# Low halves of every second weight chunk built by an accumulating transfer instead of a VectorE subtract

## The chip, the cores and the metric

One core of a Trainium2 chip runs the kernel. The metric is the device time of one execution in microseconds (us). The engines have short names in the rows: PE is TensorE (matmul), PEld its weight load, DVE is VectorE, ACT is ScalarE, POOL is GpSimd, SP is SyncE. A transfer is issued by an engine's queue (SPq, ACTq, POOLq) and carried out by the 16 DMA engines that all queues share.

## The reference

One decoder block on 256 tokens (16 meta tokens ahead of them), width 2048, in float32, with one output per token. Cut to what matters:

```
hn = rms_norm(h, norm_mix_g)
u, gb, gc, v, ga, gbr = split(hn @ w_in)
y_a = (multi_scale_pool(u) @ pool_w) * pool_scale        # 4 groups of 512 channels
y_b = (gb * causal_conv(gc * v, conv_w)) @ conv_out_w
h   = h + (sigmoid(ga + b) * y_a + sigmoid(gbr + b) * y_b) @ w_o
gate, up = split(rms_norm(h, norm_ffn_g) @ w_gate_up)    # hidden width 5632
h   = h + (silu(gate) * up) @ w_down
out = rms_norm(h, norm_final_g)[16:]
```

## The kernel before

All weights stand in memory as one stream of 528 chunks, in the order of use. A chunk is 128 partitions by 1024 float32 (512 KB), or eight tiles of 128x128. Each chunk goes through three pools: `raw` as it was loaded, `hi`, the same values rounded to float32r, and `lo = raw - hi`, the rest, also float32r. A product in nearly full precision is then three matmuls: activation hi times weight hi, activation hi times weight lo, activation lo times weight hi. In `mm_rows` a chunk is two blocks of 128x512, each used for two halves of the tokens, so 12 matmuls, and the second matmul of a chunk is the first to read `lo`. In `mm_flat` (the first stages) it is the third of 24.

`next_block` and `next_tile` hand out the tiles. At the first tile of chunk c they call `advance(c)`, which issues the load of chunk c + 4 on SP's queue and the split of chunk c + 2: ScalarE casts raw to hi (line 115), VectorE subtracts hi from raw into lo (line 116). With three buffers in `whi` and `wlo`, the split of chunk c + 2 takes the buffers of chunk c - 1, so its cast waits until TensorE has done its last matmul on chunk c - 1. `wraw` has five buffers.

The stages, in chunks: w_in in columns (0 to 127; pool and convolution branches), then gates, pool_w and conv_out_w in blocks of rows, w_o, gate and up of the FFN up to chunk 439, and w_down in four groups of 22 chunks (440 to 527), whose first group is `first` in line 451. After each group the sums in PSUM are taken over by VectorE and ScalarE (sigmoid, square, transposes and casts), and in w_down GpSimd multiplies the sum `hn` by `gf` (line 469) after the first three of the four groups. GpSimd also issues five transfers in its queue: `hn`, four of `sp` (line 384), `gf` (line 455).

Every engine takes its instructions in order: what stands behind a waiting instruction on its queue waits too. The order on each queue is made when the kernel is built, from the order in which the code records instructions.

Of the kernel before, what the change touches and what calls it, by code (L numbers as in the profile page):

```python
# [8 lines left out]
F32 = mybir.dt.float32  # L9
F32R = mybir.dt.float32r  # L10
AF = mybir.ActivationFunctionType
ALU = mybir.AluOpType
PSUM = bass.MemoryType.PSUM

P = 128
# [14 lines left out]
CH = 8  # L30
HEAD = CH // 2
LOADS_AHEAD = 4
SPLITS_AHEAD = 2

# [1 line left out]
BC = BW * P  # L38
# [15 lines left out]
def block_kernel(ctx: ExitStack, tc: tile.TileContext, xT, xn, gfin, consts, spread, weights, out):  # L54
# [4 lines left out]
    nc = tc.nc  # L59

    one = ctx.enter_context(tc.tile_pool(name="one", bufs=1))
    apool = ctx.enter_context(tc.tile_pool(name="apool", bufs=1))
    wraw = ctx.enter_context(tc.tile_pool(name="wraw", bufs=5))
    whi = ctx.enter_context(tc.tile_pool(name="whi", bufs=3))
    wlo = ctx.enter_context(tc.tile_pool(name="wlo", bufs=3))
    ps = ctx.enter_context(tc.tile_pool(name="ps", bufs=8, space=PSUM))
    scope = ExitStack()
    spool = scope.enter_context(tc.tile_pool(name="spool", bufs=KT))
# [13 lines left out]
    def bank():  # L82
        return ps.tile([P, 512], F32, name="acc")
# [8 lines left out]
    dummy = bank()  # L92
    for _ in range(WARM):
        nc.tensor.matmul(out=dummy[:, :P], lhsT=ones, rhs=ones, start=True, stop=True)
# [3 lines left out]
    raws, splits = {}, {}  # L98
# [9 lines left out]
    def split_weights(c, parts=1):  # L108
        raw = raws.pop(c)
        hi = whi.tile([P, CH * P], F32R, name="hi")  # L110
        lo = wlo.tile([P, CH * P], F32R, name="lo")
        step = CH * P // parts
        for s in range(0, CH * P, step):
            q = slice(s, s + step)
            nc.scalar.copy(out=hi[:, q], in_=raw[:, q])  # L115
            nc.vector.tensor_tensor(out=lo[:, q], in0=raw[:, q], in1=hi[:, q], op=ALU.subtract)  # L116
        splits[c] = hi, lo
# [3 lines left out]
    def advance(c):  # L121
        while state["loaded"] < min(c + LOADS_AHEAD + 1, n_chunks):
            load(state["loaded"])
            state["loaded"] += 1
        while state["split"] < min(c + SPLITS_AHEAD + 1, n_chunks):
            split_weights(state["split"])
            state["split"] += 1
# [29 lines left out]
    def rows(acts, held=0, n=None, before=None):  # L157

        ps_ = [bank() for _ in range(NB)]
        n = n or len(acts)
        for k in range(n - held):
            if before and k == n - BW:
                before()
            blk = next_block()
            for b in range(NB):
                mm_rows(ps_[b], acts[k], b, blk, k == 0, k == n - 1)
        kept = []
        for k in range(n - held, n):  # L170
            kept.append(next_block())
            mm_rows(ps_[0], acts[k], 0, kept[-1], k == 0, k == n - 1)
        for k, blk in zip(range(n - held, n), kept):
            mm_rows(ps_[1], acts[k], 1, blk, k == 0, k == n - 1)
        return ps_
# [32 lines left out]
    def binary(o, a, b, op=ALU.mult):  # L208
        nc.vector.tensor_tensor(out=o, in0=a, in1=b, op=op)
        return o  # L210
# [81 lines left out]
    for c in range(KT * HEAD // CH):  # L292
        k0 = c * CH // HEAD
        k1 = k0 + CH // HEAD
        xsp += [wide(xall[:, k, :], col(C_GMIX, k)) for k in range(k0, k1)]
        split_weights(c, 2 if c == 0 else 1)
        state["split"] = c + 1
        for k in range(k0, k1):
            for m in range(HEAD):
                cc, i = divmod(state["tile"], CH)  # L300
                state["tile"] += 1
                hi, lo = splits[cc]
                hi, lo = hi[:, i * P : (i + 1) * P], lo[:, i * P : (i + 1) * P]
                p, a, f, last = heads[m][:, : SEQ + w0], xsp[k], NMETA - w0, k == KT - 1
                nc.tensor.matmul(out=p, lhsT=hi, rhs=a[:, 0, f:], start=k == 0, stop=False)  # L305
                nc.tensor.matmul(out=p, lhsT=hi, rhs=a[:, 1, f:], start=False, stop=False)  # L306
                nc.tensor.matmul(out=p, lhsT=lo, rhs=a[:, 0, f:], start=False, stop=last)  # L307
# [57 lines left out]
    tmr = scope.enter_context(tc.tile_pool(name="tmr", bufs=1))  # L365
# [4 lines left out]
    def turn_s(c):  # L370
        turn(s_rows.pop(c), c, lambda j, p: ss.append(narrow(p, "a")))

    def gates(bias):
        gs = []
        for b, p in enumerate(rows(xsp)):
            g = slot("x", [P, BC])
            nc.vector.scalar_tensor_tensor(out=g, in0=p, scalar=r1p[:, b : b + 1], in1=bias, op0=ALU.mult, op1=ALU.add)
            nc.scalar.activation(out=g, in_=g, func=AF.Sigmoid)
            gs.append(g)
        return gs  # L380

    for c in range(NC):
        sp = tmr.tile([P, 3, BC], F32, name="sp", tag="sp", bufs=2)
        nc.gpsimd.dma_start(out=sp, in_=spread[:, :, c * BC : (c + 1) * BC])
        ga = gates(sp[:, 0, :])
        for g in ga:
            binary(g, g, sp[:, 2, :])
        if c > 0:
            turn_s(c - 1)
        gb = gates(sp[:, 1, :])  # L390
        for b, p in enumerate(rows(pooled[c * GT : (c + 1) * GT])):
            binary(ga[b], p, ga[b])
        for b, p in enumerate(rows(zs)):
            binary(gb[b], p, gb[b])
            binary(gb[b], gb[b], ga[b], ALU.add)
        s_rows[c] = gb
# [4 lines left out]
    tmr = scope.enter_context(tc.tile_pool(name="tmr", bufs=1))  # L401
# [60 lines left out]
    for c in range(NC):  # L462
        q = slice(c * BC, (c + 1) * BC)
        last = c == NC - 1
        for b, p in enumerate(first if c == 0 else rows(acts, HELD if last else 0)):
            h = hn[:, b, q]
# [21 lines left out]


HELD = 6  # L490
WARM = 14


# [70 lines left out]
```

## Time and profile before

| | |
|---|---|
| median of 2 runs | 1497.62 us (1497.62 to 1497.63) |
| the profiled execution, its own time | 1497.58 us |
| its span, first to last instruction | 1495.8 us |
| TensorE busy, share of the span | 1484.4 us, 99% |
| VectorE, ScalarE, GpSimd busy | 861.2, 657.2, 16.2 us |

The profiled execution takes 1.8 us more than its span, for what lies ahead of the first and behind the last instruction. The busy share is not the limit by itself; which wait ends last is read from the chain of waits and from the order of time.

### The profile page before, as it was taken

What the parts mean: (1) busy time and instruction counts of PE and PEld (TensorE: products, weight loads), DVE (VectorE), ACT (ScalarE), POOL (GpSimd) and SP (SyncE); (2) the same over time, 40 slices, a digit from 0 to 9 for tenths busy, and PEclk for the clock granted to TensorE, in tenths of its full rate; (3) what the DMA queues carried; (4) which work ended last, traced back from release to release, by engine and by line L of the source; (5) the groups of instructions that cost most, each with busy time, mean ns of one, the idle gap of its engine ahead of it and who ended that gap; (6) DMA issues with size and microseconds to landing.
All of it is one profiled execution on the core that took longest, in us unless ns stands there. A gap on an engine that the chain in (4) does not pass through costs nothing.

```text
span 1495.8 us, 19632 instructions
## 1 busy us (share of the span) xinstructions
PE 1484.4 (99%) x7800; PEld 1278.0 (85%) x7800; DVE 861.2 (58%) x1020; ACT 657.2 (44%) x785; POOL 16.2 (1%) x19
## 2 busy tenths in 40 slices
PE   9999999999999999999999999999999999999997
PEld 9999999999888888888888888888888888888886
DVE  7986666666555555555564555555555554445454
ACT  6444444444444444444553444444444444344343
POOL 0000000000000000000000000000000000000000
PEclk9999999999999999999999999999999999999999
DMA  8555555555765655555556555565555556556653
GB/s 340 185 179 187 185 183 184 185 185 187 231 209 183 212 184 189 191 186 191 186 169 202 192 183 194 185 189 193 192 187 189 191 185 222 183 196 197 191 192 125
DMA packets 79291, 288.76 MB, mean 193 GB/s; under 512 B 8784, under 2 KB 9040, under 8 KB 78944
## 3 DMA queue, kind: packets, MB, share of 16 engines
q1 hardware_dynamic: 77472, 279.61, 56.9%
q0 software_dynamic: 1152, 6.33, 1.3%
q8 instruction: 61, 1.00, 0.3%
q10 hardware_dynamic: 576, 1.57, 0.3%
q14 instruction: 30, 0.25, 0.0%
HBM read 285.38 MB, written 2.10 MB: 192 GB/s over the span
## 4 chain that ended last, share of the span: by engine, by line
PE 99%; ACT 0%; DMA 0%; DVE 0%; issue 0%; POOLq 0%; ACTq 0%
PE acc L155 24%; PE acc L154 24%; PE acc L153 24%; PE acc L185 6%; PE acc L187 6%; PE acc L186 6%; PE acc L179 4%; PE acc L180 2%; PE acc L242 1%; PE acc L305 1%; PE acc L307 1%; PE acc L306 1%; DMA cst<-consts 0%; ACT hi L115 0%; ACT hg L486 0%
## 5 line engine op out<-in xcount | busy, mean ns | idle before, releaser
L116 DVE TENSOR_TENSOR lo<-raw,hi 128x1024 fp32r<-128x1024 f32 (+1 forms) x529 | 648.0, 1225 | 584.2 <-ACT hi L115 581.0
L115 ACT CAST hi<-raw 128x1024 fp32r<-128x1024 f32 (+1 forms) x529 | 555.8, 1051 | 800.2 <-PE acc L155 561.7
L153 PE MATMUL acc<-hi,hp 128*128 128x512 f32 x704 | 274.7, 391 | 0.3 <-ACT hi L115 0.3
L154 PE MATMUL acc<-lo,hp 128*128 128x512 f32 x704 | 273.7, 389 | 0.0
L155 PE MATMUL acc<-hi,hp 128*128 128x512 f32 x704 | 273.7, 389 | 0.0
L153 PE MATMUL acc<-hi,act 128*128 128x512 f32 x640 | 248.8, 390 | 0.5 <-ACT hi L115 0.5
L154 PE MATMUL acc<-lo,act 128*128 128x512 f32 x640 | 248.7, 389 | 0.0
L155 PE MATMUL acc<-hi,act 128*128 128x512 f32 x640 | 248.4, 389 | 0.0
L185 PE MATMUL acc<-xp,hi 128*128 128x258 f32 (+3 forms) x704 | 200.5, 285 | 0.0
L187 PE MATMUL acc<-xp,lo 128*128 128x258 f32 (+3 forms) x704 | 199.8, 284 | 0.0
L186 PE MATMUL acc<-xp,hi 128*128 128x258 f32 (+3 forms) x704 | 198.4, 282 | 0.0
L155 PEld LDWEIGHTS acc<-hi,hp 128*128 128x128 f32 x704 | 132.1, 188 | 27.7
L153 PEld LDWEIGHTS acc<-hi,hp 128*128 128x128 f32 x704 | 132.1, 188 | 27.4 <-ACT hi L115 0.5
L154 PEld LDWEIGHTS acc<-lo,hp 128*128 128x128 f32 x704 | 132.2, 188 | 27.1
L153 PEld LDWEIGHTS acc<-hi,act 128*128 128x128 f32 x640 | 120.0, 188 | 25.9 <-ACT hi L115 1.0
L154 PEld LDWEIGHTS acc<-lo,act 128*128 128x128 f32 x640 | 120.1, 188 | 25.1
L155 PEld LDWEIGHTS acc<-hi,act 128*128 128x128 f32 x640 | 120.1, 188 | 24.7
L186 PEld LDWEIGHTS acc<-xp,hi 128*128 128x128 f32 x704 | 132.9, 189 | 0.0
L185 PEld LDWEIGHTS acc<-xp,hi 128*128 128x128 f32 x704 | 132.2, 188 | 0.7
L187 PEld LDWEIGHTS acc<-xp,lo 128*128 128x128 f32 x704 | 132.4, 188 | 0.0
L155 PE MATMUL acc<-hi,xp 128*128 128x512 f32 x256 | 101.7, 397 | 0.0
L154 PE MATMUL acc<-lo,xp 128*128 128x512 f32 x256 | 101.1, 395 | 0.0
(107 smaller groups left out, 1005.9 us busy)
## 6 DMA issues: line engine op xcount, KB each, us to landing
raw<-weights SPq DMA_DIRECT2D x527, 512.0 KB, 3.4
sp<-spread POOLq DMA_DIRECT2D x4, 768.0 KB, 6.7
hn<-xn POOLq DMA_DIRECT2D x1, 2048.0 KB, 9.8
xall<-xT SPq DMA_DIRECT2D x7, 272.0 KB, 6.8
gf<-gfin POOLq DMA_DIRECT2D x1, 1024.0 KB, 7.9
out<-hg SPq DMA_DIRECT2D x2, 512.0 KB, 2.6
out<-hg ACTq DMA_DIRECT2D x2, 512.0 KB, 3.5
raw<-weights ACTq DMA_DIRECT2D x2, 256.0 KB, 4.1
```

The source lines that it names most:

```text
L115: nc.scalar.copy(out=hi[:, q], in_=raw[:, q])
L116: nc.vector.tensor_tensor(out=lo[:, q], in0=raw[:, q], in1=hi[:, q], op=ALU.subtract)
L153: nc.tensor.matmul(out=p, lhsT=a[:, 0, t], rhs=hi, start=first, stop=False)
L154: nc.tensor.matmul(out=p, lhsT=a[:, 0, t], rhs=lo, start=False, stop=False)
L155: nc.tensor.matmul(out=p, lhsT=a[:, 1, t], rhs=hi, start=False, stop=last)
L179: nc.tensor.matmul(out=p, lhsT=hi, rhs=a[:, :, off : off + SEQ], start=first, stop=False)
L180: nc.tensor.matmul(out=p[:, :SEQ], lhsT=lo, rhs=a[:, 0, off : off + SEQ], start=False, stop=last)
L185: nc.tensor.matmul(out=p, lhsT=hi, rhs=a[:, 0, off : off + n], start=first, stop=False)
L186: nc.tensor.matmul(out=p, lhsT=hi, rhs=a[:, 1, off : off + n], start=False, stop=False)
L187: nc.tensor.matmul(out=p, lhsT=lo, rhs=a[:, 0, off : off + n], start=False, stop=last)
L242: nc.tensor.transpose(out=p[:, q : q + P], in_=src[b][:, f], identity=ident)
L305: nc.tensor.matmul(out=p, lhsT=hi, rhs=a[:, 0, f:], start=k == 0, stop=False)
```

## The change

For odd chunks from chunk 16 on (`ADD_FROM`), the low part is made in another way. ScalarE casts raw to hi as before, then ScalarE writes lo = -hi, and GpSimd's queue issues a transfer that reads the same chunk from memory a second time and adds it onto lo. Even chunks, and the first 16, keep VectorE's subtract. The splits now run three chunks ahead, `whi` and `wlo` have four buffers, `wraw` four, and `sp` one buffer instead of two.

```
-SPLITS_AHEAD = 2
+SPLITS_AHEAD = 3
...
-    wraw = ctx.enter_context(tc.tile_pool(name="wraw", bufs=5))
-    whi = ctx.enter_context(tc.tile_pool(name="whi", bufs=3))
-    wlo = ctx.enter_context(tc.tile_pool(name="wlo", bufs=3))
+    wraw = ctx.enter_context(tc.tile_pool(name="wraw", bufs=4))
+    whi = ctx.enter_context(tc.tile_pool(name="whi", bufs=4))
+    wlo = ctx.enter_context(tc.tile_pool(name="wlo", bufs=4))
...
         hi = whi.tile([P, CH * P], F32R, name="hi")
         lo = wlo.tile([P, CH * P], F32R, name="lo")
+        if c >= ADD_FROM and c % 2:
+
+            nc.scalar.copy(out=hi, in_=raw)
+            nc.scalar.activation(out=lo, in_=hi, func=AF.Copy, scale=-1.0)
+            nc.gpsimd.dma_start(out=lo, in_=weights[c], accum_op=ALU.add)
+            splits[c] = hi, lo
+            return
         step = CH * P // parts
...
-        sp = tmr.tile([P, 3, BC], F32, name="sp", tag="sp", bufs=2)
+        sp = tmr.tile([P, 3, BC], F32, name="sp", tag="sp", bufs=1)
...
+ADD_FROM = 16
```

GpSimd's queue before, from the load of `hn` to the end (L384 and L455 are the loads of `sp` and `gf`, L469 the multiplications in w_down; a row with x6 is six such instructions):

```order
L403 DMA hn<-xn 128x4096
L384 DMA sp<-spread 128x3x512 x4
L455 DMA gf<-gfin 128x2048
L469 TENSOR_TENSOR hg<-hn,gf 128x512 x6
```

The same queue after, from the last load of `sp` (now L391) to the end (L116 is the accumulating transfer, L462 the load of `gf`, L476 the multiplications):

```order
L391 DMA sp<-spread 128x3x512
L116 DMA lo<-weights 128x1024 x122
L462 DMA gf<-gfin 128x2048
L116 DMA lo<-weights 128x1024 x11
L476 TENSOR_TENSOR hg<-hn,gf 128x512 x2
L116 DMA lo<-weights 128x1024 x11
L476 TENSOR_TENSOR hg<-hn,gf 128x512 x2
L116 DMA lo<-weights 128x1024 x11
L476 TENSOR_TENSOR hg<-hn,gf 128x512 x2
L116 DMA lo<-weights 128x1024 x10
```

256 accumulating transfers now stand in a queue that had five other transfers and six multiplications. Counted from the front, those of chunks up to 439 stand ahead of the load of `gf`, and that of chunk 441 right behind it. Those of chunks 463, 485 and 507 stand right behind a pair of multiplications.

ScalarE's queue after, at the end of the first group of w_down (L122 casts an even chunk, L114 casts an odd one, L115 writes its negative into lo, L475 squares a finished sum):

```order
L122 CAST hi<-raw 128x1024
L114 CAST hi<-raw 128x1024
L475 ACTIVATE junk,part<-hn 128x512
L115 ACTIVATE lo<-hi 128x1024
L475 ACTIVATE junk,part<-hn 128x512
L122 CAST hi<-raw 128x1024
L114 CAST hi<-raw 128x1024
L115 ACTIVATE lo<-hi 128x1024
```

Per pair of chunks ScalarE has three instructions on weights instead of two. At the end of a group, work on the finished sums can stand between an odd chunk's cast and its negative; that is so in 16 places for sigmoids and squares.

## Rows read from the trace of the kernel before

**Rows 1.** The page: span, busy time, TensorE's clock, queues, the chain that ended last.
```profile
span 1495.8 us, 19632 instructions
...
PE 1484.4 (99%) x7800; PEld 1278.0 (85%) x7800; DVE 861.2 (58%) x1020; ACT 657.2 (44%) x785; POOL 16.2 (1%) x19
...
q1 hardware_dynamic: 77472, 279.61, 56.9%
...
PE 99%; ACT 0%; DMA 0%; DVE 0%; issue 0%; POOLq 0%; ACTq 0%
```

**Rows 2.** The page's costliest groups: the subtract and the cast of a chunk.
```profile
L116 DVE TENSOR_TENSOR lo<-raw,hi 128x1024 fp32r<-128x1024 f32 (+1 forms) x529 | 648.0, 1225 | 584.2 <-ACT hi L115 581.0
L115 ACT CAST hi<-raw 128x1024 fp32r<-128x1024 f32 (+1 forms) x529 | 555.8, 1051 | 800.2 <-PE acc L155 561.7
```

**Rows 3.** Windows, instructions of line 115 alone: start:end, length, ScalarE busy (casts), clock, DMA.
```profile
115.00:375.00 260.00, 95.58 (x91) 1.00 0.56 185
...
785.00:1240.00 455.00, 173.06 (x164) 1.00 0.58 190
```

**Rows 4.** Order of time, TensorE in the FFN: start, length (us), line, operands.
```profile
1015.83 0.39 PE L155 MATMUL acc<-hi,hp 128*128 128x512 f32 x1
1016.05 0.39 PE L153 MATMUL acc<-hi,hp 128*128 128x512 f32 x1
1016.28 0.39 PE L154 MATMUL acc<-lo,hp 128*128 128x512 f32 x1
```

**Rows 5.** Order of time, ScalarE in the same stretch.
```profile
1016.25 1.05 ACT L115 CAST hi<-raw 128x1024 fp32r<-128x1024 f32 x1 [1.67 <-PE acc L155]
1018.97 1.05 ACT L115 CAST hi<-raw 128x1024 fp32r<-128x1024 f32 x1 [1.67 <-PE acc L155]
```

**Rows 6.** Order of time, VectorE in the same stretch.
```profile
1017.34 1.22 DVE L116 TENSOR_TENSOR lo<-raw,hi 128x1024 fp32r<-128x1024 f32 x1 [1.49 <-ACT hi L115]
```

**Rows 7.** The page's transfers: size each, median us from issue to landing.
```profile
raw<-weights SPq DMA_DIRECT2D x527, 512.0 KB, 3.4
sp<-spread POOLq DMA_DIRECT2D x4, 768.0 KB, 6.7
hn<-xn POOLq DMA_DIRECT2D x1, 2048.0 KB, 9.8
...
gf<-gfin POOLq DMA_DIRECT2D x1, 1024.0 KB, 7.9
```

**Rows 8.** The tile sp alone: landing, shortest, median, longest.
```profile
DMA to landing us min/median/max: 5.7/6.7/11.2
```

**Rows 9.** Windows, all engines; the last three columns are clock, DMA share, GB/s.
```profile
10.00:20.00 10.00, 10.00 (x85) 10.00 (x85) 10.00 (x17) 10.00 (x20) 0.00 (x0) 1.00 1.03 416
...
1450.00:1496.00 46.00, 37.33 (x165) 30.59 (x163) 20.58 (x28) 16.11 (x20) 0.00 (x0) 0.93 0.39 137
```

**Rows 10.** Order of time, GpSimd in the FFN's end and w_down.
```profile
1246.85 0.55 POOL L455 DMA_DIRECT2D gf<-gfin  x1 [751.86 <-DVE gs L447]
1309.08 3.54 POOL L469 TENSOR_TENSOR hg<-hn,gf 128x512 f32<-128x512 f32 x2 [61.68 <-DVE hn L209]
1367.96 3.53 POOL L469 TENSOR_TENSOR hg<-hn,gf 128x512 f32<-128x512 f32 x2 [55.35 <-DVE hn L209]
1427.81 3.54 POOL L469 TENSOR_TENSOR hg<-hn,gf 128x512 f32<-128x512 f32 x2 [56.31 <-DVE hn L209]
```

**Rows 11.** Order of time, TensorE where w_down begins.
```profile
1246.15 0.39 PE L155 MATMUL acc<-hi,hp 128*128 128x512 f32 x1
1246.38 0.39 PE L153 MATMUL acc<-hi,act 128*128 128x512 f32 x1
```

**Rows 12.** Order of time, VectorE where w_down begins.
```profile
1246.09 1.40 DVE L447 SCALAR_TENSOR_TENSOR gs<-acc,r,gs 128x512 f32<-128x512 f32 x2
```

**Rows 13.** Order of time, TensorE at the end of w_down's first group.
```profile
1308.33 0.39 PE L155 MATMUL acc<-hi,act 128*128 128x512 f32 x1
1308.56 0.39 PE L154 MATMUL acc<-lo,act 128*128 128x512 f32 x1
```

**Rows 14.** Order of time, ScalarE at the same place.
```profile
1308.80 1.05 ACT L115 CAST hi<-raw 128x1024 fp32r<-128x1024 f32 x1 [1.67 <-PE acc L155]
1309.76 0.63 ACT L468 ACTIVATE junk<-hn 128x512 f32<-128x512 f32 x1
...
1311.05 0.19 ACT L468 ACTIVATION_READ_ACCUMULATOR junk<-hn 128x1 f32 x1
```

## The prediction

> **What bounds the kernel now.** I read the page first, then the chain of waits that ended last, then the order of time in one quiet stretch of the FFN, then every transfer that GpSimd issues, since the change gives that queue 256 more. TensorE is busy for 99% of the span and is 99% of the chain; VectorE, which the change relieves, is busy for 58% and has no share in the chain worth a percent [rows 1]. The subtract costs 1.225 us and the cast 1.051 us per chunk, and each stands behind long idle times of its engine that end with its predecessor, not with a lack of its own time [rows 2]. So taking 256 subtracts (256 x 1.225 = 314 us) off VectorE shortens nothing that ends last. There is at most about 1% (the share of TensorE not busy) to gain, less than the 2% that a measurement of this kernel can tell from no change. The question is only whether the new way of making lo is in time.
>
> **The beat and the budget.** In the FFN 164 chunks take 455 us, with the transposes in them; in the first stages 91 chunks take 260 us, 2.86 us each [rows 3]. The quiet beat is the distance of two casts, 18.97 - 16.25 = 2.72 us [rows 5]. Follow one chunk boundary: the last matmul of a chunk starts at 1015.83, the first of the next at 1016.05, the first that needs lo at 1016.28 [rows 4]. The cast that waited for the released buffer starts at 1016.25, 0.20 us behind the boundary, and ends at 1017.30 [rows 5]; VectorE's subtract starts at 1017.34 [rows 6] and ends at 1018.56. With three buffers that chunk is first used two beats behind the boundary, at 1021.5: 2.9 us to spare.
>
> After the change, an odd chunk n gets the buffers of chunk n - 4, three beats ahead of its use: 3 x 2.72 = 8.16 us, plus 0.23 until its first matmul with lo (1016.28 - 1016.05), so lo must have landed 8.39 us behind the boundary. Out of that: 0.20 until the cast, 1.05 the cast, 0.04 handover, 1.05 the new negative (no row shows it; I take the cast of the same 128x1024 on the same engine, bounds 1.0 and 1.3, the subtract being the other row of that size), and 0.06 until GpSimd issues (the load of gf starts at 1246.85 [rows 10], the first of VectorE's two instructions of 0.70 us from 1246.09 ends at 1246.79 [rows 12]). That is 2.40, so **6.0 us remain** from the issue of the accumulating transfer to its landing. Call that time X. In the first stages, where a beat is 2.86, the budget is 6.0 + 3 x 0.14 = 6.4.
>
> If X is longer, the loop boundary, cast, negative, transfer, use, boundary is longer than four beats, and nothing takes that up: four chunks then take 10.88 + (X - 6.0). No loads further ahead help, because the buffer, not the data, starts the chain.
>
> **The price X.** No row shows an accumulating transfer. From below: a plain load of the same 512 KB on SP's queue lands after 3.4 us [rows 7]. From above: 2048 KB on GpSimd's queue took 9.8 us [rows 7], and the longest `sp` 11.2 [rows 8]. Between: 768 KB on GpSimd's queue 5.7 at the least and 6.7 in the median [rows 7, 8], 1024 KB 7.9 [rows 7]. An accumulate onto lo must read 512 KB of weights and also the 512 KB that stand in lo, so it reads 1 MB like gf, but writes only 512 KB. I take 7.0, between sp and gf. All of these ran beside the weight loads, as the accumulates will; the DMA engines' total says the same. Plain loads move 416 GB/s when the engines are full [rows 9], that is 1.26 us for a chunk, 2.5 us for the two loads of a pair of chunks in 5.44 us. An accumulate at twice the price of a load adds 2.5: 5.0 of 5.44, nearly full, so queueing is to be expected and no transfer comes at its best time.
>
> The Trainium skill ("DMA: Bandwidth & Descriptors", Anatomy of one DMA) fits a GpSimd transfer by 2.0 us plus bytes over 436 GB/s; an estimate from it for 512 KB is 3.2 us, which would put X far inside the budget. The trace here does not agree for this queue: the same fit gives 4.4 us for gf, and its row says 7.9 [rows 7]. The skill's page "Collectives: The Full Stack" (Part 3, why ReduceScatter is half of AllGather) says that an add in the DMA needs two source reads and so halves the rate; no run here shows it so far, and by it X would be near gf's 7.9 and the steady term below 190 instead of 100.
>
> **The sum**, against the profiled execution's 1497.58 us (the median of the runs is 1497.62):
> - Steady loop, chunks 128 to 527: 100 groups of four, each 7.0 - 6.0 = 1.0 longer: 100 us. Chunks 16 to 127: 28 groups, 0.6 each: 17 us.
> - GpSimd's queue in w_down. The multiplications wait for VectorE's last sum of a group and run until 1309.08 + 3.54 = 1312.62 [rows 10]. The accumulate of chunk 463 stands behind them and is issued at 1312.67 at the earliest; the boundary is at 1308.56 [rows 13], so its lo is needed at 1308.56 + 2.72 + 0.23 = 1311.51. It lands at 1319.7, 8.2 late; about 1.0 of that is in the steady term, so 7. Three such places (the three pairs last the same [rows 10]): 21 us.
> - The load of gf waits for VectorE until 1246.85 and holds the queue until 1247.40 [rows 10]; the accumulate of chunk 441 stands behind it. It is needed 2.95 us behind the boundary of 1246.38 [rows 11], at 1249.33, and lands between 1254.4 and, if gf's own megabyte goes first, 1257: 5 to 8 late, 7 us.
> - ScalarE at the end of groups: squares or sigmoids now stand between an odd cast and its negative. In w_down the cast ends at 1309.85 and the squares at 1311.24 [rows 14], so the negative is 1.3 us later; in 16 places, 21 us.
> - At no cost: 256 negatives on ScalarE (269 us) bring its 657 us [rows 1] to 926, under 60% of the longer span; odd casts that follow wait for buffers anyhow [rows 2]. The fourth `wraw` buffer instead of the fifth: a raw load still starts over four beats (10.9 us) ahead of its cast and lands in 3.4 [rows 7]. If loads took three times as long in the fuller queue, this cover would be gone and X would lengthen the beat once more. `sp` with one buffer is read a full eight chunks (22 us) behind its issue.
>
> 100 + 17 + 21 + 7 + 21 = 166: **1664 us**, 11% slower. At 1.0 us more of X the sum is 128 higher, which is why the range is wide. TensorE's waits may also cost clock: the stretch in which it is busy for 37 of 46 us has 0.93 of the clock granted, elsewhere 1.00 [rows 9]. No row shows waits of 0.5 us or of 8 us in the middle of the work, so I add nothing for it; after the four long ones a few us more are possible, inside the range.
>
> **The rivals.**
> *The transfer is hidden* (not slower). If an accumulate costs the engines what a plain load costs, X is 4.0 to 5.2, between the raw load's 3.4 and sp's least of 5.7. Then the steady loop has slack and swallows ScalarE's 1.3 us too. What stays is the queue order of w_down: with X = 4.5, 1312.67 + 4.5 - 1311.51 = 5.7 at three places and about 5.4 behind gf, 22 us: 1520, 1.5% above and inside 2%. It decides for X below about 5.2. For it: 512 KB is less than any transfer of that queue that the rows show. Against it: the second read, and the fuller engines. This is also the result by the skill's fit.
>
> *The DMA engines become the bound.* If an accumulate costs more than 5.44 - 2.5 = 2.9 us of all engines, 2.3 times a load, the pair of chunks takes as long as its transfers. At four times, 2.5 + 5.0 = 7.5 per pair: 200 x 2.1 + 56 x 1.8 + 28 = 550, or 2045. X by then is near hn's 9.8, and the loop alone would say the same (100 x 3.8 + 28 x 3.4 + 49 = 524). For it: nothing in the trace excludes a slow adder. Against it: nothing shows one.
>
> *It gains.* TensorE would have to get faster by 2% through a quieter VectorE; its matmuls stand at even distances of 0.22 to 0.23 us [rows 4], whatever VectorE does, so I give this next to nothing.
>
> **How the numbers follow.** Forecast (X from 5.5 to 8.5, 1550 to 1860 as its own range): 0.57. Hidden: 0.22, with about 1520. DMA-bound: 0.19, from 1860 to 2060. Gain: 0.02. The range from 1515 to 1880 leaves out most of the DMA-bound case, the gain, and little of the rest: 0.2 together. Slower by over 2% is the forecast and the DMA-bound case and the upper part of the hidden one (X from 4.8 to 5.5 gives 1527 to 1550): 0.82. Within 2%: 0.16. Faster: 0.02.
>
> **What the profile after would show.** Accumulates that land after some 7 us; TensorE's idle time in front of the second matmul of odd chunks, released by the transfer, about 0.5 us each; ScalarE's casts of a group of four 11.9 us apart instead of 10.9; three waits of 7 to 9 us some 58 us apart at the end, behind the multiplications; TensorE's busy share near 90%; about 420 MB in all. If accumulates land in under 6 us, the steady term falls away and I am wrong by 100 us; if the DMA share is near 1.0 throughout and raw loads are late too, the engines are the bound and I am wrong the other way.

## The result and the profile after

| | before | after |
|---|---|---|
| median | 1497.62 us | 1719.16 us (1717.15 to 1721.17, 2 runs) |
| span of the profiled execution | 1495.8 us | 1719.4 us |
| mean granted clock of TensorE | 0.998 | 0.983 |

The ratio is 1.148, 95% interval 1.1454 to 1.15: slower by 222 us. The forecast was 1664 with a range from 1515 to 1880, so the direction, the loop as the mechanism and the range held. The increase was forecast as 166 us, and its make-up did not hold: the two terms of the steady loop were about half of what they measured, the two of GpSimd's queue were not there, and that of ScalarE is not isolated.

The page of the changed kernel, the lines that answer to [rows 1]:

```profile
span 1719.4 us, 20130 instructions
...
PE 1559.9 (91%) x7800; PEld 1289.3 (75%) x7800; DVE 559.3 (33%) x764; ACT 917.6 (53%) x1041; POOL 236.5 (14%) x275
...
q0 software_dynamic: 38016, 140.57, 47.4%
q1 hardware_dynamic: 77472, 279.61, 45.0%
...
DMA 45%; PE 41%; ACT 9%; issue 4%; DVE 1%; POOL 0%; POOLq 0%; ACTq 0%
...
L116 POOL DMA_DIRECT2D lo<-weights x256 | 223.2, 872 | 1410.2 <-ACT lo L115 1162.1
...
raw<-weights SPq DMA_DIRECT2D x527, 512.0 KB, 5.4
lo<-weights POOLq DMA_DIRECT2D x256, 512.0 KB, 7.3
```

VectorE is down to 559 us, as the change means, and TensorE's share is 91% instead of 99%. The chain that ended last used to be TensorE alone; now 45% of it is the landing of accumulating transfers, and 9% ScalarE's cast and negative. The landing X took 7.3 us in the median (forecast 7.0, budget 6.0). Raw loads land after 5.4 us instead of 3.4 [rows 7]. GpSimd's queue q0 has half as many packets as q1 and holds the 16 DMA engines longer.

The chain around one accumulate, from the chain of waits in a stretch of the FFN (start, length, what):

```profile
1156.78 0.24 PE acc L162
1157.02 0.02 issue
1157.04 1.06 ACT hi L114
1158.10 0.02 issue
1158.12 1.07 ACT lo L115
1159.19 0.28 issue
1159.48 8.68 DMA lo<-weights
1168.16 0.04 issue
1168.20 0.50 PE acc L161
```

This is the loop that the prediction drew, link by link: the last matmul on the buffer, cast, negative, issue, landing, and the second matmul of the odd chunk three beats later. Two things differ: the link into the queue is 0.28 us from the negative's end to the issue, where I had 0.06, and this landing, 8.68 us, is one of the longer ones (nine in ten take less than 8.1). The same wait in the order of time of TensorE:

```profile
1159.56 0.39 PE L160 MATMUL acc<-hi,hp 128*128 128x512 f32 x1
1161.64 0.50 PE L161 MATMUL acc<-lo,hp 128*128 128x512 f32 x1 [1.69 <-DMA lo<-weights]
...
1166.99 0.39 PE L160 MATMUL acc<-hi,hp 128*128 128x512 f32 x1
1168.20 0.50 PE L161 MATMUL acc<-lo,hp 128*128 128x512 f32 x1 [0.82 <-DMA lo<-weights]
```

The first matmul of an odd chunk (hi) runs, the second (lo) waits for the landing, here 1.69 and 0.82 us. In the whole trace TensorE stands idle for a landing 151 times, 149 us in all. The other 75 us of the longer span are in its busy time [rows 1]: records that elsewhere overlap (0.39 us long, 0.23 apart) stand alone at a wait, and some ran at a lower clock, as shown further down.

How much longer a group of four chunks became, by windows with the negatives of line 115 alone (one per pair of chunks; start:end, length, ScalarE busy, clock, DMA share, GB/s):

```profile
115.00:375.00 260.00, 43.25 (x41) 1.00 0.96 250
...
850.00:1400.00 550.00, 90.20 (x85) 0.98 0.93 244
```

In the FFN 85 pairs take 550 us, 12.94 per group of four; before, 164 chunks took 455, 11.10 per group [rows 3]: 1.84 longer. In the first stages 260 / 41 x 2 = 12.68 against 11.43 [rows 3]: 1.25 longer. Over 100 and 28 groups that is 184 + 35 = 219 us, nearly the whole increase of 222. The casts themselves say the same: from that of chunk 17 to that of chunk 527 it takes 218 us longer than before. These windows hold the ends of groups too, with ScalarE's squares and sigmoids.

### The profile page after: what moved, and what is told of

It is laid out like the page before. It is cut to its first block, busy times and chain, and to the rows that moved or that the text cites. A ratio compares the mean times of both kernels' runs of the same rounds, so it can differ in the third digit from the quotient of the medians.

```text
span 1719.4 us, 20130 instructions
## 1 busy us (share of the span) xinstructions
PE 1559.9 (91%) x7800; PEld 1289.3 (75%) x7800; DVE 559.3 (33%) x764; ACT 917.6 (53%) x1041; POOL 236.5 (14%) x275
## 3 DMA queue, kind: packets, MB, share of 16 engines
q0 software_dynamic: 38016, 140.57, 47.4%
## 4 chain that ended last, share of the span: by engine, by line
DMA 45%; PE 41%; ACT 9%; issue 4%; DVE 1%; POOL 0%; POOLq 0%; ACTq 0%
DMA lo<-weights 45%; PE acc L161 11%; PE acc L162 10%; PE acc L160 9%; ACT lo L115 4%; ACT hi L114 4%; PE acc L194 2%; PE acc L193 2%; PE acc L192 2%; PE acc L186 1%; PE acc L187 1%; PE acc L249 1%; PE acc L313 0%; PE acc L312 0%; PE acc L314 0%
## 5 line engine op out<-in xcount | busy, mean ns | idle before, releaser
L123 DVE TENSOR_TENSOR lo<-raw,hi 128x1024 fp32r<-128x1024 f32 (+1 forms) x273 | 333.4, 1221 | 946.2 <-ACT hi L122 946.0
L114 ACT CAST hi<-raw 128x1024 fp32r<-128x1024 f32 x256 | 269.0, 1051 | 604.5 <-PE acc L162 473.2
L116 POOL DMA_DIRECT2D lo<-weights x256 | 223.2, 872 | 1410.2 <-ACT lo L115 1162.1
L122 ACT CAST hi<-raw 128x1024 fp32r<-128x1024 f32 (+1 forms) x273 | 284.5, 1043 | 132.1 <-PE acc L162 104.0
L161 PE MATMUL acc<-lo,hp 128*128 128x512 f32 x704 | 285.2, 405 | 53.7 <-DMA lo<-weights 53.5
L161 PE MATMUL acc<-lo,act 128*128 128x512 f32 x640 | 261.7, 409 | 52.8 <-DMA lo<-weights 52.5
L160 PE MATMUL acc<-hi,hp 128*128 128x512 f32 x704 | 279.0, 397 | 0.0
L162 PE MATMUL acc<-hi,hp 128*128 128x512 f32 x704 | 278.9, 396 | 0.0
L115 ACT ACTIVATE lo<-hi 128x1024 fp32r<-128x1024 f32 x256 | 271.2, 1059 | 6.4
L162 PE MATMUL acc<-hi,act 128*128 128x512 f32 x640 | 256.2, 400 | 0.0
L160 PE MATMUL acc<-hi,act 128*128 128x512 f32 x640 | 255.9, 400 | 0.0
L192 PEld LDWEIGHTS acc<-xp,hi 128*128 128x128 f32 x704 | 132.9, 189 | 0.7
```

The lines of the kernel that those rows point to most:

```text
L114: nc.scalar.copy(out=hi, in_=raw)
L115: nc.scalar.activation(out=lo, in_=hi, func=AF.Copy, scale=-1.0)
L116: nc.gpsimd.dma_start(out=lo, in_=weights[c], accum_op=ALU.add)
L160: nc.tensor.matmul(out=p, lhsT=a[:, 0, t], rhs=hi, start=first, stop=False)
L161: nc.tensor.matmul(out=p, lhsT=a[:, 0, t], rhs=lo, start=False, stop=False)
L162: nc.tensor.matmul(out=p, lhsT=a[:, 1, t], rhs=hi, start=False, stop=last)
```

## The experiments

Theories: the *loop* theory (four chunks take as long as one round from buffer release to landing and use), the *full engines* theory (the 16 DMA engines have no more to give), and with the loop two views of X: the landing takes 7 us of its own, or it is stretched by the raw loads beside it. All ratios are to the kernel before, run on the same chip.

**The pools alone, with the subtract.**
```
-ADD_FROM = 16
+ADD_FROM = 10000
```


> The pools of the change (four hi and lo buffers, four raw, one sp, splits three ahead), but VectorE subtracts every chunk. Loop theory (a beat of four chunks waits for cast, negative and landing): no transfer is waited for, 1495 to 1503. Rival (the smaller raw pool or the single sp buffer costs): over 1520.

Measured 1496.33 us, ratio 0.9994 (0.9985 to 1.0003). The smaller raw pool, the single `sp` buffer and the three chunks ahead cost and gain nothing, so all 222 us belong to the accumulating path. This run keeps VectorE's subtracts; that its 314 us were not on TensorE's way is read from the chain, of which TensorE is 99% [rows 1].

**A plain transfer instead of the accumulating one.** lo here holds the whole chunk, not its low part.
```
-            nc.gpsimd.dma_start(out=lo, in_=weights[c], accum_op=ALU.add)
+            nc.gpsimd.dma_start(out=lo, in_=weights[c])
```


> The change with a plain transfer in place of the accumulating one: same queue, same bytes from memory, same waits, but lo is overwritten with the whole chunk instead of getting the rest. Loop theory: packets of 159 ns instead of 328, landing about 5 us, inside the 6.0 that the loop allows: 1500 to 1535. Rival (GpSimd's queue itself is late, whatever the transfer does): landing still about 7 us, over 1650. Full-engines theory (the 16 DMA engines have no more to give): a pair has 2.5 + 1.3 us of transfers in 5.44, so also about 1500.

Measured 1526.39, ratio 1.019 (1.0174 to 1.0206): slower, but not clear of 2%. Its page:

```profile
q0 software_dynamic: 38016, 140.57, 28.9%
...
L116 POOL DMA_DIRECT2D lo<-weights x256 | 135.8, 530 | 1305.4 <-ACT lo L115 1015.7
...
lo<-weights POOLq DMA_DIRECT2D x256, 512.0 KB, 4.9
```

The same queue, the same packets and bytes: 28.9% of a span of 1520.4 is 439 us of all engines, 47.4% of 1719.4 is 815. With the addition the packets take 1.9 times as long, and the landing 7.3 instead of 4.9. GpSimd's own instruction takes 872 ns instead of 530, so a third of a microsecond of those 2.4 is the issue; the rest comes with the addition and not with the queue. That it is the second read, and not the adding, no run separates. The Trainium skill ("Collectives: The Full Stack", Part 3, why ReduceScatter is half of AllGather) says that an add in the DMA needs two source reads and halves the rate; the factor of 1.9 in these two runs agrees with it. Its other figure ("DMA: Bandwidth & Descriptors", Anatomy of one DMA), by which 512 KB would take an estimated 3.2 us, does not hold beside the weight loads, where the plain transfer took 4.9 in the median (3.3 at the least).

**All the work, but nobody waits for it.** The accumulate goes into a spare tile, with three hi and lo buffers and the splits two ahead, as in the kernel before.
```
-SPLITS_AHEAD = 3
+SPLITS_AHEAD = 2
...
+            nc.vector.tensor_tensor(out=lo, in0=raw, in1=hi, op=ALU.subtract)
+            side = wside.tile([P, CH * P], F32R, name="side")
-            nc.scalar.activation(out=lo, in_=hi, func=AF.Copy, scale=-1.0)
-            nc.gpsimd.dma_start(out=lo, in_=weights[c], accum_op=ALU.add)
+            nc.scalar.activation(out=side, in_=hi, func=AF.Copy, scale=-1.0)
+            nc.gpsimd.dma_start(out=side, in_=weights[c], accum_op=ALU.add)
```


> Everything that the change issues (second cast on ScalarE, accumulating transfer), but into a spare tile that nobody reads; lo comes from VectorE's subtract for all chunks, with three hi and lo buffers and splits two ahead as before. Loop theory: the bytes do no harm unless they are waited for, 1497 to 1520, with raw loads landing in 5 to 6 us and the accumulates in about 7. Full-engines theory: as slow as the change, about 1700, with casts that wait for raw loads.

Measured 1498.49, ratio 1.0012 (1.0002 to 1.0021). Its page:

```profile
DMA  8799999999999999999999999999999999999998
...
raw<-weights SPq DMA_DIRECT2D x527, 512.0 KB, 6.6
side<-weights POOLq DMA_DIRECT2D x256, 512.0 KB, 8.2
```

The engines are busy throughout, at a higher pace than in the change, and transfers land later than I had expected (8.2 us instead of about 7, raw loads 6.6 instead of 5 to 6), yet the kernel takes the time of before. This is the cleanest run of the study: the transfers, the second pass of ScalarE and GpSimd's issues are free; only waiting for them is not. The full-engines theory falls.

**Five buffers, splits four ahead.** `wlo` has five as well, the loads run five ahead, and to make room there are three raw buffers and eight in the ring.
```
-SPLITS_AHEAD = 3
+SPLITS_AHEAD = 4
...
-    whi = ctx.enter_context(tc.tile_pool(name="whi", bufs=4))
+    whi = ctx.enter_context(tc.tile_pool(name="whi", bufs=5))
...
```


> The change with five hi and lo buffers and splits four ahead (three raw buffers and eight ring buffers to make room). Loop theory: the budget from issue to landing grows by a beat, 6.0 + 2.7 = 8.7 us, over the median of 7.3; only the longest landings (10 us) still stall: 1505 to 1570. Full-engines theory: the same transfers take the same time, 1680 to 1720.

Measured 1542.94, ratio 1.032 (1.0278 to 1.0361): 176 us less than the change although X is no shorter (7.5 in the median).

The list of waits (us in total, times, longest), first of the change, then of this run:

```profile
ACT hi L114 <- PE acc L162: 473.2, 186, 7.7
PEld acc L161 <- DMA lo<-weights: 180.9, 139, 4.8
```
```profile
ACT hi L114 <- PE acc L162: 109.8, 68, 4.5
...
PEld acc L161 <- DMA lo<-weights: 36.8, 36, 3.7
```

Odd casts wait for TensorE to release a buffer 68 times instead of 186, and TensorE's weight loads wait for landings 36 times instead of 139. What is left has another source, a line of the same list:

```profile
ACT hi L114 <- DMA raw<-weights: 326.1, 147, 6.3
```

With three raw buffers the casts wait for raw loads. The control:

> The buffers of the run with five (three raw, eight in the ring, splits four ahead), but VectorE subtracts every chunk: what making room costs by itself. 1497 to 1510 if it costs nothing; over 1520 if casts wait for raw loads.

The same pools with the subtract took 1503.05, ratio 1.0034 (1.0021 to 1.0047): making room costs 6 us by itself, and presumably more beside the accumulates, where raw loads land in 5.9 us instead of 3.3.

**The loop's links.** Three runs that make one link shorter or longer, with four buffers.
```
-            nc.scalar.activation(out=lo, in_=hi, func=AF.Copy, scale=-1.0)
+            nc.vector.tensor_scalar(out=lo, in0=hi, scalar1=-1.0, scalar2=None, op0=ALU.mult)
```


> The change with the negative of hi made by VectorE instead of ScalarE. Loop theory: the negative of 128x1024 takes VectorE between 0.6 and 1.2 us instead of 1.06, and stands behind no squares or sigmoids on ScalarE any more; up to 0.45 us less per group of four (128 x 0.45 = 58) and up to 20 for the 16 places: 1640 to 1715. Rival (VectorE's copy holds up GpSimd, which writes the transfer's descriptors): landing later than 7.3 us, 1720 or more.

Measured 1702.85, ratio 1.1387 (1.1341 to 1.1433). VectorE's negative took 0.70 us instead of 1.06, but the landing 7.4 (in the mean 7.36 instead of 7.09): 16 us less, inside the range, where 0.36 x 128 = 46 and the places at the ends of groups were to be had.

```
             nc.scalar.activation(out=lo, in_=hi, func=AF.Copy, scale=-1.0)
+            nc.scalar.activation(out=lo, in_=hi, func=AF.Copy, scale=-1.0)
```


> The change with the negative written twice by ScalarE, which is idle for 47% of the change's span: one link of the loop longer by 1.06 us. Loop theory: every group of four chunks longer by that, 128 x 1.06 = 136: 1820 to 1875. Full-engines theory: the engines have the same work, ScalarE has room, 1715 to 1735.

Measured 1736.22, ratio 1.1579 (1.1541 to 1.1618): 17 us more, not 136. A miss for the loop theory as I had written it. The tile lo in this run, shortest, median and longest landing:

```profile
DMA to landing us min/median/max: 5.1/5.5/10.5
```

The median fell by 1.8 us. For a loop that runs 256 times the mean counts, and by the trace it fell from 7.09 to 6.00: issued 1.1 us later, the transfers landed at the same moment. So X is not a price of the transfer alone. In the change an odd cast frees its raw buffer, SP issues the next raw load 0.03 us later, and the accumulate is issued some 1.4 us behind that. The idea is that it waits for that load's packets; the run with the raw load moved tests it.

```
+            for s in range(0, CH * P, CH * P // 2):
+                q = slice(s, s + CH * P // 2)
+                nc.scalar.copy(out=hi[:, q], in_=raw[:, q])
+                nc.scalar.activation(out=lo[:, q], in_=hi[:, q], func=AF.Copy, scale=-1.0)
+                nc.gpsimd.dma_start(out=lo[:, q], in_=weights[c, :, q], accum_op=ALU.add)
```


> The change with cast, negative and accumulate in two halves of 512 columns each: the same bytes, twice the instructions. Loop theory: the first half is issued about 1.1 us earlier and is half as long, the second half is not needed until the seventh matmul of the chunk, 1.4 us later: about 1 us less per group, 1570 to 1650. Full-engines theory: 1700 to 1740; rival (GpSimd's issue, 0.87 us each, now 1.75 per odd chunk) slower than 1720.

Measured 1617.40, ratio 1.0796 (1.0761 to 1.0831): 102 us less, inside the loop theory's band. Twice the issues on GpSimd cost less than the halves gained.

**The raw load moved out of the way.** The miss above asked for this run: no instruction of the loop is shortened, only the competing load is held back, by a one-column addition that still reads the odd raw tile after the next even subtract.
```
+            held_raw.append(raw)
...
+        if held_raw:
+            nc.vector.tensor_tensor(out=hold, in0=held_raw.pop()[:, :1], in1=lo[:, :1], op=ALU.add)
         splits[c] = hi, lo
```


> The change, except that an odd chunk's raw buffer is held until VectorE has subtracted the next even chunk (an addition of one column that reads it), so that the raw load which reuses it starts some 4 us later, with the next one, instead of 1.4 us ahead of the accumulate. Same bytes, same links of the loop. If the landing is set by what lies ahead of and between the accumulate's packets (raw loads): landing 5 to 6 us instead of 7.1 on average, 1520 to 1620. If the 7 us are the accumulate's own, or GpSimd's issue: landing as before, 1700 to 1740. A raw load that comes too late for its cast would show as casts waiting for raw.

Measured 1586.11, ratio 1.0576 (1.0542 to 1.061): 133 us less. Its page:

```profile
q0 software_dynamic: 38016, 140.57, 48.8%
...
raw<-weights SPq DMA_DIRECT2D x527, 512.0 KB, 5.2
lo<-weights POOLq DMA_DIRECT2D x256, 512.0 KB, 5.5
```

Same bytes, same links, and the landing falls from 7.3 to 5.5 in the median, from 7.09 to 5.87 in the mean. So 1.2 us of X, and with it 60% of the loss, hung on the raw load's place just ahead of the accumulate. The traces say how far ahead: the last raw load is issued 1.4 us before the accumulate in the change, 1.0 with VectorE's negative, and 2.4 here and with the doubled negative; the median landings are 7.3, 7.4, 5.5 and 5.5. What stays argued is by which way the nearness costs. In the change the accumulate ahead is also still under way at 73% of the issues, here at 41%, and the transfers may hold each other up.

**An accumulate for every fourth chunk.**
```
-        if c >= ADD_FROM and c % 2:
+        if c >= ADD_FROM and c % 4 == 1:
```


> The change with an accumulate for every fourth chunk only, VectorE's subtract for the others. Full-engines theory: a group of four has 7.7 us of transfers in 10.9, so nothing is late: 1497 to 1515. Loop theory: the group still waits for one landing through the same buffer, with the same two raw loads beside it; landing 6 to 7 us against a budget of 6.0, so up to 1.0 per group of four: 1510 to 1640.

Measured 1601.62, ratio 1.0691 (1.0647 to 1.0735). Window 850 to 1300 us, all engines:

```profile
850.00:1300.00 450.00, 427.93 (x1888) 347.22 (x1887) 176.33 (x187) 221.21 (x244) 32.93 (x38) 1.00 0.78 221
```

Half the accumulates, 78% of the engines' time instead of 93%, and still 104 us lost: one late landing per round is enough. X was 6.3 in the median and in the mean, with the raw load 1.4 us ahead as in the change but no accumulate under way at any issue: so the raw load's place is not all that lengthens X.

**GpSimd's queue cleared.** The multiplications of w_down go to VectorE, the load of gf to SP's queue.
```
-    nc.gpsimd.dma_start(out=gf, in_=gfin)
+    nc.sync.dma_start(out=gf, in_=gfin)
...
-            (nc.vector if last else nc.gpsimd).tensor_tensor(out=hg[:, b, q], in0=h, in1=gf[:, q], op=ALU.mult)
+            nc.vector.tensor_tensor(out=hg[:, b, q], in0=h, in1=gf[:, q], op=ALU.mult)
```


> The change with nothing but accumulates on GpSimd's queue in w_down: the multiplications of line 476 go to VectorE, the load of gf to SP's queue. As the prediction had it (accumulates held up by 7 us at four places): 28 less, 1688 to 1695. By the trace after (the accumulates right behind them are those of chunks 443, 465, 487 and 509, a pair later than counted, and are hardly held up): 0 to 8 less, 1710 to 1720.

Measured 1713.53, ratio 1.1452 (1.1418 to 1.1485), not told apart from the change: the queue's order cost nothing that can be measured.

**Three shortenings together**: two halves, the raw load held back, the negative by VectorE (the edits above).

> The three shortenings of the loop in one kernel, with four buffers as in the change: two halves (102 less on their own), the odd chunk's raw load held back (133 less), the negative by VectorE (16 less). If each takes a part of the same overrun, 1497 to 1530, the floor being what TensorE needs; if they only add up to what the engines' work allows (5.2 of 5.44 us per pair, with queueing), 1520 to 1570. Not faster than the kernel before in either case, since TensorE is the bound there.

Measured 1573.40, ratio 1.0497 (1.0472 to 1.0522), only 13 us better than the held-back load alone, and just above both ranges that I had given. Its page and its list of waits:

```profile
raw<-weights SPq DMA_DIRECT2D x527, 512.0 KB, 6.3
lo<-weights POOLq DMA_DIRECT2D x512, 256.0 KB, 6.6
```
```profile
ACT hi L118 <- DMA raw<-weights: 82.5, 36, 3.6
```

The gains do not add up. The halves land later again (6.6 us for half the size), and now casts wait for raw loads as well. How much of that rest is the held-back load coming late, and how much the queueing of transfers that all want to go earlier, was not separated.

## Why the prediction was right, and where it was not

**Nothing to gain on VectorE: right.** The pools without the accumulate run like the kernel before, and the change freed VectorE of a third of its busy time for nothing.

**The loop and its budget: right.** Five buffers took back 176 us with landings as long as before, and the same work unwaited cost nothing; the chain after shows each link.

**X = 7.0: right in size (7.3 in the median, 7.1 in the mean), wrong in kind.** I argued from what an accumulate must read, and the shorter landing of the plain transfer fits that. But I treated X as a constant, so that "at 1.0 us more of X" or of any link "the sum is 128 higher". The doubled negative (17 us instead of 136) shows that the constant does not exist: the landing is set partly by the raw loads beside it, and issuing 1.1 us later did not land later. That the 7.0 came out is partly luck: with the raw load 2.4 us ahead instead of 1.4 the same transfer took 5.9 in the mean, and the prediction had no view of that distance. I had said that queueing was to be expected, and did not draw the time of the raw load into the loop, though it is issued by the very cast that starts it.

**The steady term, 117 us, is the mis-sized one: it measured 219.** Per group in the FFN I had 1.0 and it was 1.84. The trace accounts for most of it, in means over the odd chunks: X longer by 0.1 (7.09), the negative 0.12 later behind the cast (0.16 instead of 0.04), the issue 0.25 later (0.31 instead of 0.06), 0.04 from the landing to the matmul and 0.11 because the first matmul after a wait takes 0.50 instead of 0.39. The 0.06 was read from a plain load behind VectorE; behind VectorE's negative an accumulate is issued after 0.29 in the median. Then there is the clock, which I left at nothing, having no row of waits in the middle of the work. In one stretch of the changed kernel:

```profile
470.00:490.00 20.00, 17.09 (x63) 13.54 (x62) 3.82 (x4) 8.43 (x8) 1.72 (x2) 0.83 0.83 225
```

TensorE's order of time at that place:

```profile
473.33 0.39 PE L160 MATMUL acc<-hi,act 128*128 128x512 f32 x1
476.62 0.79 PE L161 MATMUL acc<-lo,act 128*128 128x512 f32 x1 [2.91 <-DMA lo<-weights]
477.22 0.63 PE L162 MATMUL acc<-hi,act 128*128 128x512 f32 x1
```

It had waited 2.91 us for a landing, and the matmuls behind the wait took 0.79 and 0.63 us instead of 0.39: part of the stretch ran at the lower level of 1.2 GHz, hence 0.83 on average. Over the span the mean clock is 0.983 against 0.998: 0.015 x 1719 = 26 us at most, 0.2 per group. All of these make about 0.8 of the missing 0.84. This is an estimate: not every round waits for its landing (151 of 256), landings spread from 5.2 to 10.0 us, and no run separates the shares.

**The queue in w_down, 28 us: wrong.** I counted the accumulates ahead of gf one short. Right behind gf and the multiplications stand chunks 443, 465, 487 and 509, whose negatives are not ready any earlier. GpSimd after, at the first group's end:

```profile
1500.75 2.54 POOL L476 TENSOR_TENSOR hg<-hn,gf 128x512 f32<-128x512 f32 x2 [3.99 <-DVE hn L216]
1503.39 0.89 POOL L116 DMA_DIRECT2D lo<-weights  x1
```

ScalarE's negative for that accumulate, in its own order of time:

```profile
1502.06 1.04 ACT L115 ACTIVATE lo<-hi 128x1024 fp32r<-128x1024 f32 x1
```

It ends at 1503.10 and the transfer is issued 0.29 later, as anywhere else. TensorE's longest wait for a landing behind one of the four is 2.5 us, where 7 to 9 were forecast. The sentences of the section on the change that name chunks 439, 441, 463, 485 and 507 are off by this one pair.

**ScalarE at the ends of groups, 21 us: not isolated.** The delays are there. The negative of chunk 443 starts 1.42 us behind its cast, those of 465, 487 and 509 0.52 to 0.53, where 0.03 is usual; over all odd chunks they come to some 30 us. But they lie inside the windows of the loop, so they are part of its 219 us and not a term beside it, and what of them reached TensorE no run isolates: taking the negative off ScalarE gave 16 us for both its effects.

So the sum came near for a partly wrong reason. 28 us that were not there and 21 that belong to the loop stood in for about half of the 102 that the loop was short, and that is luck.

**The rivals.** The hidden transfer is excluded by its condition: the accumulate does not cost what a plain load costs. With the plain transfer's 4.9 the kernel came to 1526, near the 1520 of that rival, but not through the queue of w_down: of the 25 us by which its profiled execution is longer, 21 lie between chunks 129 and 439, and 4 in w_down. The DMA engines as the bound are excluded by the unwaited run and by the every-fourth run. A gain through VectorE is excluded by the chain, and by the plain transfer, where VectorE is as free (555 us) and TensorE's busy time is no shorter (1493 us against 1484).

## What to carry to other kernels

Before moving work off an engine that is not in the chain, draw the loop that the new way closes (buffer release to next use) and count its beats against the buffers; a long-latency link costs every round what it overruns, however idle the engines are, and a buffer more can be worth more than a shorter link (here 176 us against 16, 102 and 133). Do not price a transfer's landing as a constant: look for what issues the transfers that run beside it, because a load that is freed by the same instruction can run just ahead of it. And in a loop count with the mean of a landing, not with its median.

## What the runs showed of the hardware

- An accumulating transfer onto SBUF holds the DMA engines 1.9 times as long as a plain one of the same packets (47.4% of 1719.4 us against 28.9% of 1520.4), and lands after 7.3 instead of 4.9 us here. In the unwaited run the same packets take 49.8% of 1495.5, 1.7 times the plain ones.
- Issued 1.1 us later it landed after 6.0 us instead of 7.1 in the mean (5.5 instead of 7.3 in the median): the moment of landing did not move with the moment of issue.
- At a DMA share of 1.00 and 283 GB/s over the whole span of the unwaited run, with landings of 6.6 and 8.2 us, TensorE lost nothing as long as no wait depended on the late half.
- The pair of multiplications on GpSimd took 2.54 us instead of 3.54 [rows 10] in the change, where VectorE has fewer subtracts to do beside it. The Trainium skill ("SBUF — State Buffer", Who interferes with whom) says that a VectorE instruction with two SBUF inputs contends with GpSimd's reads; these two rows fit that, as does the run of the pools alone (1.79 us for one of the pair, as before). The run with five buffers has as few subtracts as the change and took 1.63, so the cause is not shown.
